# An encoder block on one core: four diagonals for the row of silu(c), h of a group made during the group ahead, modulation tiles spread one behind a weight tile, six half tiles in the ring

## The chip, the core and the metric

The kernel runs on one core of a Trainium2 chip. The metric is device time in microseconds (us) of one execution: 1720.41 us, the median of three runs (1719.41 to 1721.68). Five engines work side by side, each through its own queue in order: PE (matrix products; PEld is its weight load), DVE and ACT (elementwise), POOL (idle here) and SP, which here issues DMAs only.

## The reference, cut to what matters

```
mod = silu(c) @ W_ada + b_ada          # six rows of 2048: sh1, sc1, gt1, sh2, sc2, gt2
h   = rmsnorm(x, g_pre_mix) * (1 + sc1) + sh1          # x is 256 x 2048
proj = h @ w_in                        # 2048 x 10752: HGRN2 q, f, b, v, g; attention q, k, v; gates a, b
y = (sigmoid(gate_a) * (hgrn2(..) @ w_branch_a) + sigmoid(gate_b) * (attention(..) @ w_branch_b)) @ w_out
x = x + gt1 * rmsnorm(y, g_post_mix)
h = rmsnorm(x, g_pre_ffn) * (1 + sc2) + sh2
x = x + gt2 * rmsnorm(16 experts, each on the 32 tokens it picks, g_post_ffn)
```

All weights come from HBM once, in float32.

## The kernel before, in words

**Tiles.** Every weight is cut into tiles of 128 x 2048 float32 (1 MB). `stream` lists them in the order of `prog`, and `take` gives each a slot of `Mem` and issues its DMA on SP. `Mem` has 27 slots of 8 KB a partition, for tiles of weights and for everything else, handed out in the order in which they were freed in the program; a DMA waits until the slot's last user is through.

**Two sorts of tiles in the front part.** A modulation tile ("A" for sh1 and sc1, "B" for the other four rows) is used once on DVE: `ada` (L392) multiplies it by CR, the row of silu(c), and sums. A weight tile ("W" for w_in, "YA", "YB", "O" for the branch and output weights) is split by `split` into a high part (ACT, L426) and a rest (DVE, L427), in two halves. A half takes a slot of a ring (`NHL` of the 27 slots, 4 here). `finish` multiplies: 48 products 256 columns wide, or 24 of 512. It runs `LAH` weight tiles behind the split, 1 here.

**Order of the work.** CR is made first (`expand`: four times a diagonal on DVE L282, a product with ones on PE, a copy on ACT L293; one buffer for the diagonal), then x is normed and transposed into nT. h is made by `make_h` in four groups of four 128-row blocks, since the first ten chunks of w_in ("early": f0, b0, f1, b1, q0, q1, hg0, hg1, v0, v1) are gone through once for each group. Between groups the partial sums rest in SBUF: ACT copies them out of PSUM (L783) and in again (L780). h of a group needs its eight A tiles: `mod_gain` (L397, L399), then scale (ACT L409), high part (ACT L410) and rest (DVE L411). At a group's head the program finishes all products in flight before it makes h. After the groups come 44 "late" weight tiles, in whose time HGRN2 and then attention run as generators (`run_bg`, four steps after each weight tile), then 32 tiles of the branches and of the output (`dlist`). Before: in groups 0 to 2 eight A tiles among the first nine weight tiles, in group 3 eight B tiles; 38 B tiles among the late ones; the last 18 in the first 18 of `dlist`.

**Experts.** After a short stretch of norms and routing on small tiles, 16 experts of 24 tiles each are streamed through.

A scheduler puts the instructions into the engines' queues, so that their order differs a little from the program's.

Of the kernel before, what the change touches and what calls it, by code (L numbers as in the profile page):

```python
# [14 lines left out]
F32 = mybir.dt.float32  # L15
# [11 lines left out]
H = 8  # L27
# [3 lines left out]
EPS = 1e-6  # L31
ATT_SCALE = 128 ** -0.5
NEG = -3.0e38
BL = 0.87
BE = 8
BD = 18
NHL = 4
BG = 4
GRP = [4, 4, 4, 4]
NA0 = 1  # L40
HK = 1
LAH = 1


COLS = {}
# [80 lines left out]
def block_kernel(ctx: ExitStack, tc: tile.TileContext, x, cols, pos, ident_in, hmask, smask, w_ada, w_in, w_a, w_b, w_out, w_r, w_gu, w_dn, out):  # L126
    nc = tc.nc
    V, S, E = nc.vector, nc.scalar, nc.tensor
# [3 lines left out]
    mem = Mem(sp, 27)  # L132
    hring = Ring(mem, NHL)
    PS = pp.tile([128, 4096], F32, name="PS")
# [8 lines left out]
    def bank():  # L143
        ring["m"] = (ring["m"] + 1) % 3
        return PS[:, 2048 + 512 * ring["m"]:2560 + 512 * ring["m"]]
# [18 lines left out]
    pairs = []  # L164

    def latest(engine):
        for i in reversed(nc.cur_bb.bb.instructions):
            if i.engine == engine:
                return i
# [8 lines left out]
    def mm(o, l, r, start, stop, **kw):  # L178
        E.matmul(o, l, r, start=start, stop=stop, skip_group_check=True, **kw)  # L179
# [7 lines left out]
    def col(n, a=0, b=None):  # L187
        lo, hi = COLS[n]
        t, o = (ct0, 0) if lo < NCOL0 else (ct, NCOL0)
        return t[:, lo - o + a:(hi if b is None else lo + b) - o]  # L190
# [15 lines left out]
    def tiny(n):  # L206
        a = spos[0]
        spos[0] += n
        assert spos[0] <= SMW
        return small[:, a:a + n]  # L210

    def table(name="natural_log_exp_and_others"):

        S.preload_act_table_set(name)

    def rsqrt(ss, n):

        l, r, t, v = tiny(n), tiny(n), tiny(n), tiny(n)
        S.activation(l, ss, AF.Ln, scale=1.0 / D, bias=epsc)
        S.activation(r, l, AF.Exp, scale=-0.5)  # L220
        V.tensor_scalar(v, ss, 1.0 / D, EPS, ALU.mult, ALU.add)
        V.tensor_tensor(t, r, r, ALU.mult)
        V.scalar_tensor_tensor(t, t, -0.5, v, ALU.mult, ALU.mult)
        V.scalar_tensor_tensor(r, t, 1.5, r, ALU.add, ALU.mult)
        return r


    NG = len(GRP)
    G0 = [sum(GRP[:g]) for g in range(NG)]
    prog = [("X",)]  # L230
    a_tiles = [("A", p, k) for k in range(KT) for p in range(2)]
    b_tiles = [("B", p, k) for p in range(2, 6) for k in range(KT)]
    prog += a_tiles[:2 * GRP[0]]
    for g in range(NG):
        prog.append(("H", g))
        if g < NG - 1:
            todo = a_tiles[2 * G0[g + 1]:2 * G0[g + 1] + 2 * GRP[g + 1]]
        else:
            todo = b_tiles[:BE]
            b_tiles = b_tiles[BE:]  # L240
        nt, ne = len(todo), len(EARLY)
        for i, n in enumerate(EARLY):
            prog.append(("W", n, G0[g], GRP[g]))
            k = min(nt, (i + 1) * nt // (ne - NA0)) - min(nt, i * nt // (ne - NA0))
            prog += todo[:k]
            todo = todo[k:]
        prog += todo
    def mix(items, n, m):

        nonlocal prog, b_tiles  # L250
        n = min(n, len(b_tiles))
        for i, it in enumerate(items):
            prog.append(it)
            k = min(n, (i + 1) * n // m) - min(n, i * n // m)
            prog += b_tiles[:k]
            b_tiles = b_tiles[k:]

    late = [("W", n, 4 * q, 4) for n in LATE for q in range(4)]
    mix(late, int(BL * len(late) + 0.5), len(late))
    dlist = []  # L260
    for c in range(4):
        dlist += [("YA", c, q) for q in range(2)] + [("YB", c, q) for q in range(2)]
    dlist += [("O", c, q) for c in range(4) for q in range(4)]
    mix(dlist, len(b_tiles), BD)

    def src(it):
        k = it[0]
# [12 lines left out]
    def spread(c4, w, b=None):  # L280

        V.tensor_tensor(w, ident[:, None, :].to_broadcast([128, 4, 128]),  # L282
                        c4[:, :, None].to_broadcast([128, 4, 128]), ALU.mult)
        b = bank() if b is None else b
        mm(b, ones, w.rearrange("p a b -> p (a b)"), True, True)
        return b

    def expand(c16, name):

        r = mem.get([D], F32, name)  # L290
        w = mem.get([4, 128], F32, "diag")
        for c in range(4):
            S.copy(r[:, 512 * c:512 * c + 512], spread(c16[:, 4 * c:4 * c + 4], w))  # L293
        mem.put(w)
        return r

# [5 lines left out]
    def hk(tl, kt):  # L302
        return tl[kt // 8][:, kt % 8, :]
# [3 lines left out]
    S.activation(sig, col("c"), AF.Sigmoid)  # L307
    V.tensor_tensor(sig, sig, col("c"), ALU.mult)
    CR = expand(sig, "crow")
    X = [mem.get([D], F32, "x") for _ in range(NT)]  # L310
    ssq = tiny(NT)

    def norm_x():
        for tt in range(NT):
            nc.sync.dma_start(X[tt], x[tt])
        scr = mem.get([D], F32, "sq")
        for tt in range(NT):
            S.activation(scr, X[tt], AF.Square, accum_out=ssq[:, tt:tt + 1])
        mem.put(scr)
        rs = rsqrt(ssq, NT)  # L320
        for k2 in range(8):
            if k2 % 2 == 0:
                for tt in range(NT):
                    xp = X[tt][:, 256 * k2:256 * k2 + 512]
                    S.activation(xp, xp, AF.Copy, scale=rs[:, tt:tt + 1])
            b = bank()
            for j in range(2):
                for tt in range(NT):
                    E.transpose(b[:, 256 * j + 128 * tt:256 * j + 128 * tt + 128],
                                X[tt][:, 128 * (2 * k2 + j):128 * (2 * k2 + j) + 128], ident)  # L330
            S.copy(NTl[k2 // 4][:, 2 * (k2 % 4):2 * (k2 % 4) + 2, :].rearrange("p a b -> p (a b)"), b)
        mem.put(*X)

# [56 lines left out]
    def ada(p, k, t):  # L390

        V.scalar_tensor_tensor(t, t, 1.0, CR, ALU.mult, ALU.mult, accum_out=MOD[:, p, k:k + 1])  # L392
        mem.put(t)

    def mod_gain(p, ks):
        m = MOD[:, p, ks]
        V.tensor_tensor(m, m, bada[:, p, ks], ALU.add)  # L397
        if p in (1, 4):
            V.scalar_tensor_tensor(m, m, 1.0, col("gpm" if p == 1 else "gpf")[:, ks], ALU.add, ALU.mult)  # L399
        elif p in (2, 5):  # L400
            V.tensor_tensor(m, m, col("gqm" if p == 2 else "gqf")[:, ks], ALU.mult)

    def make_h(g):
        ks = slice(G0[g], G0[g] + GRP[g])
        mod_gain(0, ks)
        mod_gain(1, ks)
        for kt in range(ks.start, ks.stop):
            n = hk(NTl, kt)
            S.activation(n, n, AF.Identity, scale=MOD[:, 1, kt:kt + 1], bias=MOD[:, 0, kt:kt + 1])  # L409
            S.copy(hk(HH, kt), n)  # L410
            V.tensor_tensor(hk(HL, kt), n, hk(HH, kt).bitcast(F32), ALU.subtract)  # L411
            if kt % 2:
                yield
        if g == NG - 1:
            mem.put(*NTl)
# [57 lines left out]
    def late_tiles(names):  # L473
        for n in names:
            OT[n] = mem.get([8, 256], F32R, n)
# [149 lines left out]
    def attn_pre():  # L625
        AQ, AKV = SL["AQ"], SL["AKV"]
        late_tiles(("BH", "BL"))
        V.memset(SC, NEG)
# [15 lines left out]
    def attn(h):  # L644
# [40 lines left out]
        S.copy(OT["BH"][:, h, :], b[:, :256])  # L685
        V.tensor_tensor(OT["BL"][:, h, :], b[:, :256], OT["BH"][:, h, :].bitcast(F32), ALU.subtract)
        yield
# [6 lines left out]
        "YA": (lambda k: OT["OH"][:, k, :], lambda k: OT["OL"][:, k, :]),  # L694
        "YB": (lambda k: OT["BH"][:, k, :], lambda k: OT["BL"][:, k, :]),
        "O": (lambda k: hk(MH, k), lambda k: hk(ML, k)),
# [71 lines left out]
    def finish(it, parts):  # L768
# [29 lines left out]
        elif k in ("YA", "YB"):  # L798
# [11 lines left out]
            if q == 1:  # L810
# [6 lines left out]
                else:  # L817
# [3 lines left out]
                    if c == 3:  # L821
                        table()
                        mem.put(OT["OH"], OT["OL"], OT["BH"], OT["BL"])
        else:
# [23 lines left out]
    last_b = [it for it in prog if it[0] == "B"][-1]  # L848
    LA = LAH
    pend = []  # L850
    hs = iter(())
    for it in prog:
        if it[0] == "H":
            while pend:
                finish(*pend.pop(0))
            hs = make_h(it[1])
            for _ in range(HK):
                next(hs)
            continue
        if it[0] == "X":  # L860
            norm_x()
            rotary()
            continue
        t = take()
        if it[0] in "AB":
            ada(it[1], it[2], t)
            if it[0] == "B" and it[2] % 4 == 3:
                mod_gain(it[1], slice(it[2] - 3, it[2] + 1))
            if it == last_b:
                mem.put(CR)  # L870
            if it == ("B", 4, KT - 1):
                router_consts()
        else:
            pend.append((it, split(t)))
            for _ in hs:
                pass
            while len(pend) > LA:
                finish(*pend.pop(0))
            run_bg(BG)
# [117 lines left out]
    for e in range(NE):  # L997
# [9 lines left out]
        for k in range(KT):  # L1007
            w = take()
# [201 lines left out]
```

## Time and profile before

| | |
|---|---|
| median of 3 runs | 1720.41 us |
| the profiled execution | 1721.07 us, its span 1719.3 us |
| PE busy | 1437.4 us (84%) |
| DVE busy / ACT busy | 775.7 us (45%) / 555.7 us (32%) |
| moved by DMA | 633.57 MB, 369 GB/s over the span |
| chain that ended last | PE 47%, DMA 44%, DVE 5%, ACT 2% |

The span is the time from the first to the last instruction; times of the trace count from its start. A share over the whole span mixes stages: the front part (to 757 us), the routing (to 790 us) and the experts. PEclk is the granted TensorE clock as a share of full speed.

### The profile page before, as it was taken

What the parts mean: (1) busy time and instruction counts of PE and PEld (TensorE: products, weight loads), DVE (VectorE), ACT (ScalarE), POOL (GpSimd) and SP (SyncE); (2) the same over time, 40 slices, a digit from 0 to 9 for tenths busy, and PEclk for the clock granted to TensorE, in tenths of its full rate; (3) what the DMA queues carried; (4) which work ended last, traced back from release to release, by engine and by line L of the source; (5) the groups of instructions that cost most, each with busy time, mean ns of one, the idle gap of its engine ahead of it and who ended that gap; (6) DMA issues with size and microseconds to landing.
All of it is one profiled execution on the core that took longest, in us unless ns stands there. A gap on an engine that the chain in (4) does not pass through costs nothing.

```text
span 1719.3 us, 21982 instructions
## 1 busy us (share of the span) xinstructions
PE 1437.4 (84%) x9114; PEld 866.6 (50%) x9114; DVE 775.7 (45%) x1060; ACT 555.7 (32%) x858; POOL 0.2 (0%) x4
## 2 busy tenths in 40 slices
PE   4999999999999999997877777776777777687777
PEld 2989998778888888862322222221222222132123
DVE  6767787999997898442111101110110111011113
ACT  6467786665565444441200100100010011001003
POOL 0000000000000000000000000000000000000000
PEclk9999999999999999998988878878897989887888
DMA  9988955787979899767999999999999999999995
GB/s 384 418 338 326 361 218 202 271 312 269 363 296 365 331 420 399 276 266 306 418 419 420 420 420 419 420 420 419 418 419 419 420 420 420 419 420 419 418 419 233
DMA packets 88659, 633.57 MB, mean 369 GB/s; under 512 B 10096, under 2 KB 10480, under 8 KB 11760
## 3 DMA queue, kind: packets, MB, share of 16 engines
q1 hardware_dynamic: 88128, 631.39, 90.7%
q8 instruction: 71, 1.16, 0.3%
q10 hardware_dynamic: 432, 0.79, 0.1%
q14 instruction: 28, 0.23, 0.0%
HBM read 630.04 MB, written 2.10 MB: 368 GB/s over the span
## 4 chain that ended last, share of the span: by engine, by line
PE 47%; DMA 44%; DVE 5%; ACT 2%; issue 1%; SPq 0%; ACTq 0%; DVEq 0%
PE PS L179 45%; DMA w<-in_w_gu_dram 34%; DMA w<-in_w_dn_dram 9%; DVE w L392 2%; DVE hl L427 1%; ACT ew L1051 1%; DMA w<-in_w_in_dram 1%; PE PS L1024 0%; DMA w<-in_w_ada_dram 0%; ACT hl L426 0%; PE PS L903 0%; ACT ew L1021 0%; DVE F L500 0%; PE PS L678 0%; PE PS L760 0%
## 5 line engine op out<-in xcount | busy, mean ns | idle before, releaser
L179 PE MATMUL PS<-w,rt 128*32 128x512 f32 x2048 | 327.2, 717 | 141.2 <-DMA w<-in_w_gu_dram 139.5
L427 DVE TENSOR_TENSOR hl<-w,hl 128x1024 fp32r<-128x1024 f32 x232 | 280.8, 1222 | 107.7 <-ACT hl L426 107.3
L179 PE MATMUL PS<-hl,hl 128*128 128x256 f32 (+1 forms) x928 | 311.5, 336 | 0.0
L426 ACT CAST hl<-w 128x1024 fp32r<-128x1024 f32 x232 | 241.7, 1050 | 157.1 <-PE PS L179 146.8
L179 PE MATMUL PS<-hl,hh 128*128 128x512 f32 x832 | 267.9, 398 | 4.0 <-DVE hl L427 4.0
L179 PEld LDWEIGHTS PS<-w,rt 128*32 128x32 f32 x2048 | 54.7, 116 | 371.3 <-DMA w<-in_w_gu_dram 305.8
L392 DVE SCALAR_TENSOR_TENSOR w<-w,crow 128x2048 f32<-128x2048 f32 x96 | 218.8, 2284 | 4.6 <-ACT crow L293 2.8
L179 PE MATMUL PS<-ew,rt 128*128 128x256 f32 x512 | 155.8, 431 | 60.1 <-ACT ew L1051 60.1
L1062 DVE TENSOR_TENSOR acc<-acc,PS 128x512 f32<-128x512 f32 x120 | 82.5, 688 | 268.6 <-PE PS L179 268.6
L179 PE MATMUL PS<-hh,hl 128*128 128x256 f32 x1024 | 189.4, 287 | 12.5 <-ACT hl L426 8.3
L179 PEld LDWEIGHTS PS<-hl,hl 128*128 128x128 f32 x928 | 178.8, 193 | 16.5 <-issue 1.0
L179 PEld LDWEIGHTS PS<-hl,hh 128*128 128x128 f32 x832 | 154.8, 188 | 37.5 <-DVE hl L427 5.9
L179 PEld LDWEIGHTS PS<-hh,hl 128*128 128x128 f32 x1024 | 163.5, 196 | 13.7 <-ACT hl L426 8.7
L179 PE MATMUL PS<-w,ew 128*32 128x256 f32 x2048 | 152.0, 420 | 13.9 <-DVE ew L1030 13.9
L179 PEld LDWEIGHTS PS<-ew,rt 128*128 128x128 f32 x512 | 93.5, 202 | 134.0 <-ACT ew L1051 119.9
L1051 ACT COPY ew<-PS 128x256 f32<-128x256 f32 x128 | 47.6, 372 | 259.2 <-PE PS L179 259.2
L1030 DVE TENSOR_TENSOR ew<-ew,PS 128x256 f32<-128x256 f32 x16 | 6.7, 422 | 234.1 <-ACT ew L1029 234.1
L963 DVE TENSOR_SCALAR rt<-ct,rt,small 128x32 f32<-128x32 f32 x32 | 9.4, 300 | 214.8 <-PE PS L179 214.7
L179 PEld LDWEIGHTS PS<-w,ew 128*32 128x32 f32 x2048 | 57.4, 117 | 87.4 <-issue 49.0
L969 ACT COPY ew<-PS 128x512 f32<-128x512 f32 x15 | 8.8, 586 | 273.4 <-PE PS L179 273.4
L1021 ACT COPY ew<-PS 128x512 f32<-128x512 f32 x16 | 9.4, 586 | 234.1 <-PE PS L179 234.1
L179 PE MATMUL PS<-hl,mh 128*128 128x512 f32 x256 | 80.9, 396 | 0.0
(242 smaller groups left out, 1114.0 us busy)
## 6 DMA issues: line engine op xcount, KB each, us to landing
w<-in_w_gu_dram SPq DMA_DIRECT2D x256, 1024.0 KB, 19.9
w<-in_w_dn_dram SPq DMA_DIRECT2D x128, 1024.0 KB, 19.9
w<-in_w_ada_dram SPq DMA_DIRECT2D x96, 1024.0 KB, 8.1
w<-in_w_in_dram SPq DMA_DIRECT2D x84, 1024.0 KB, 7.4
w<-in_w_out_dram SPq DMA_DIRECT2D x16, 1024.0 KB, 11.1
w<-in_w_a_dram SPq DMA_DIRECT2D x8, 1024.0 KB, 10.0
w<-in_w_b_dram SPq DMA_DIRECT2D x8, 1024.0 KB, 11.8
x<-in_x_dram SPq DMA_DIRECT2D x4, 1024.0 KB, 9.4
```

The lines of the kernel that those rows point to most:

```text
L179: E.matmul(o, l, r, start=start, stop=stop, skip_group_check=True, **kw)
L392: V.scalar_tensor_tensor(t, t, 1.0, CR, ALU.mult, ALU.mult, accum_out=MOD[:, p, k:k + 1])
L426: S.copy(hl[:, 0, :], w)
L427: V.tensor_tensor(hl[:, 1, :], w, hl[:, 0, :].bitcast(F32), ALU.subtract)
L963: V.tensor_scalar(oh[:, tt, :], io, pm3[:, tt, e:e + 1], r2[:, tt:tt + 1], ALU.is_equal, ALU.mult)
L969: S.copy(g, b)
L1021: S.copy(gu, b)
L1030: V.tensor_tensor(he, sl_, b3[:, :, 64:128], ALU.mult)
L1051: S.copy(EW[:, 2, 256 * (cb % 2):256 * (cb % 2) + 256], b[:, :256])
L1062: V.tensor_tensor(acc(cb), acc(cb), p3, ALU.add)
```

## The change

Four things. `expand` has a buffer for each of its four diagonals. The ring has six half tiles and `finish` runs two weight tiles behind the split. h of group g+1 is begun after the eighth weight tile of group g and goes on by two blocks with each of its last two weight tiles (`next(hs)`), with nothing flushed ahead; h of group 0 is held behind the split of the first weight tile, and the second square of x behind the copies of CR. The modulation tiles follow at most one behind a weight tile: ten in each of the four groups (8 A and 2 B, in the last 10 B), 12 behind the first 30 late tiles, 14 behind the other 14, 8 behind the first 16 of `dlist`, 14 behind the next 14.

```diff
-BL = 0.87
-BE = 8
-BD = 18
-NHL = 4
+BE = [2, 2, 2, 10]
+BL = [(30, 12), (14, 14)]
+BD = [(16, 8), (14, 14)]
+NHL = 6
-NA0 = 1
-HK = 1
-LAH = 1
+NH0 = 3
+LAH = 2
@@ prog
-        prog.append(("H", g))
+        todo = b_tiles[:BE[g]]
+        b_tiles = b_tiles[BE[g]:]
         if g < NG - 1:
-            todo = a_tiles[2 * G0[g + 1]:2 * G0[g + 1] + 2 * GRP[g + 1]]
-        else:
-            todo = b_tiles[:BE]
-            b_tiles = b_tiles[BE:]
+            todo = a_tiles[2 * G0[g + 1]:2 * G0[g + 1] + 2 * GRP[g + 1]] + todo
         for i, n in enumerate(EARLY):
             prog.append(("W", n, G0[g], GRP[g]))
-            k = min(nt, (i + 1) * nt // (ne - NA0)) - min(nt, i * nt // (ne - NA0))
+            if g == 0 and i == 0:
+                prog.append(("H", 0))
+            k = min(nt, (i + 1) * nt // ne) - min(nt, i * nt // ne)
             prog += todo[:k]
             todo = todo[k:]
+            if g < NG - 1 and i == ne - NH0:
+                prog.append(("H", g + 1))
@@ expand
-        w = mem.get([4, 128], F32, "diag")
+        w = mem.get([4, 4, 128], F32, "diag")
         for c in range(4):
-            S.copy(r[:, 512 * c:512 * c + 512], spread(c16[:, 4 * c:4 * c + 4], w))
+            S.copy(r[:, 512 * c:512 * c + 512], spread(c16[:, 4 * c:4 * c + 4], w[:, c]))
@@ norm_x
+        pairs.append((latest(mybir.EngineType.Activation), crow_done))
@@ the loop over prog
         if it[0] == "H":
-            while pend:
-                finish(*pend.pop(0))
-            hs = make_h(it[1])
-            for _ in range(HK):
-                next(hs)
+            hs, hg_ = make_h(it[1]), it[1]
+            if it[1] == 0:
...
+                for _ in hs:
+                    pass
             continue
...
             pend.append((it, split(t)))
-            for _ in hs:
-                pass
+            if it[0] == "W" and it[2] < G0[hg_]:
+                next(hs, None)
+            else:
+                for _ in hs:
+                    pass
```

**Place 1: ACT at the start.** nT holds x normed and transposed; hh is the high part of h, hl the halves of a weight tile w. Before:

```order
L331 COPY nT_82<-PS 128x512 x2
L409 ACTIVATE nT_81<-nT_81,MOD 128x256 x2
L410 CAST hh_83<-nT_81 128x256 x2
L426 CAST hl_236<-w_234 128x1024
L426 CAST hl_239<-w_234 128x1024
```

Now:

```order
L337 COPY nT_82<-PS 128x512 x2
L432 CAST hl_227<-w_225 128x1024
L432 CAST hl_230<-w_225 128x1024
L415 ACTIVATE nT_81<-nT_81,MOD 128x256 x2
L416 CAST hh_83<-nT_81 128x256 x2
L415 ACTIVATE nT_81<-nT_81,MOD 128x256 x2
L416 CAST hh_83<-nT_81 128x256 x2
```

The first weight tile's two halves went ahead of h of group 0.

**Place 2: ACT from group 0 to group 1.** Q takes the sums of v0 and then of v1, the last two chunks of group 0; F is f0's, the first chunk of group 1; w_800, w_814 and w_762 are group 1's first tiles. Before:

```order
L426 CAST hl_802<-w_800 128x1024
L410 CAST hh_83<-nT_81 128x256
L426 CAST hl_805<-w_800 128x1024
L409 ACTIVATE nT_81<-nT_81,MOD 128x256 x2
L410 CAST hh_83<-nT_81 128x256
L783 COPY Q_77_559<-PS 128x1024
L410 CAST hh_83<-nT_81 128x256
L426 CAST hl_816<-w_814 128x1024
L426 CAST hl_819<-w_814 128x1024
L780 COPY PS<-F_44_256 128x1024 x2
```

Now:

```order
L415 ACTIVATE nT_81<-nT_81,MOD 128x256
L789 COPY HG_643<-PS 128x1024
L416 CAST hh_83<-nT_81 128x256
L432 CAST hl_698<-w_696 128x1024
L432 CAST hl_701<-w_696 128x1024
L789 COPY Q_78_512<-PS 128x1024
L786 COPY PS<-F_52_270 128x1024
L432 CAST hl_764<-w_762 128x1024
L432 CAST hl_767<-w_762 128x1024
L789 COPY Q_85_573<-PS 128x1024
```

All of h now stands ahead of the last tile's split (w_696), and the copy that brings f0's sums back into PSUM ahead of the copy that takes v1's sums out.

**Place 3: SP in the output products.** Before:

```order
L160 DMA w_5356<-in_w_out_dram 128x2048
L160 DMA w_5388<-in_w_out_dram 128x2048
L160 DMA w_5420<-in_w_out_dram 128x2048
L160 DMA w_5456<-in_w_out_dram 128x2048
L160 DMA w_5491<-in_w_out_dram 128x2048
```

Now:

```order
L159 DMA w_5506<-in_w_ada_dram 128x2048
L159 DMA w_5509<-in_w_out_dram 128x2048
L159 DMA w_5541<-in_w_ada_dram 128x2048
L159 DMA w_5544<-in_w_out_dram 128x2048
L159 DMA w_5580<-in_w_ada_dram 128x2048
L159 DMA w_5585<-in_w_out_dram 128x2048
```

Twelve modulation tiles that were loaded earlier now stand between the tiles of w_out, ahead of the first expert's.

## Rows read from the trace of the kernel before

**Rows 1.** Busy time by stage; columns of all such tables in the first line.

```profile
core 0: us, PE busy (x) PEld busy (x) DVE busy (x) ACT busy (x) POOL busy (x), PEclk, DMA share, GB/s
103.00:283.00 180.00, 180.00 (x1324) 172.94 (x1324) 135.26 (x135) 131.81 (x148) 0.00 (x0) 0.98 0.78 298
283.00:400.00 117.00, 111.59 (x576) 88.89 (x575) 114.33 (x152) 76.71 (x107) 0.00 (x0) 1.00 0.70 265
400.00:520.00 120.00, 119.98 (x578) 97.05 (x577) 116.93 (x188) 73.10 (x129) 0.00 (x0) 1.00 0.79 301
667.00:757.50 90.50, 90.50 (x395) 72.88 (x394) 45.23 (x44) 36.70 (x47) 0.00 (x0) 1.00 0.73 286
757.50:790.50 33.00, 18.51 (x98) 8.44 (x102) 21.48 (x62) 11.46 (x35) 0.00 (x0) 0.74 0.71 287
850.00:1700.00 850.00, 627.25 (x4474) 212.44 (x4476) 122.17 (x212) 77.37 (x196) 0.00 (x0) 0.84 1.01 417
```

**Rows 2.** Timeline of SP, 676 to 800 us: start, length, engine, line, DMAs.

```profile
757.91 16.23 SPq L160 DMA_DIRECT2D w<-in_w_dn_dram  x8
791.45 24.16 SPq L160 DMA_DIRECT2D w<-in_w_gu_dram  x16
```

**Rows 3.** Busy time just ahead of the first expert's products.

```profile
782.00:791.00 9.00, 5.85 (x32) 1.88 (x36) 5.28 (x17) 0.96 (x2) 0.00 (x0) 0.67 0.01 5
```

**Rows 4.** Timeline of the start; idle time before and what ended it in brackets.

```profile
5.03 2.08 PE L179 MATMUL PS<-diag,ones 128*128 128x512 f32 x2 [5.03 <-DVE diag L282]
7.73 1.91 ACT L318 ACTIVATE sq<-x 128x2048 f32<-128x2048 f32 x1 [4.88 <-DMA x<-in_x_dram]
16.69 0.59 ACT L293 COPY crow<-PS 128x512 f32<-128x512 f32 x1 [2.34 <-PE PS L179]
17.31 2.29 DVE L392 SCALAR_TENSOR_TENSOR w<-w,crow 128x2048 f32<-128x2048 f32 x1 [2.77 <-ACT crow L293]
36.64 1.09 ACT L409 ACTIVATE nT<-nT,MOD 128x256 f32<-128x256 f32 x2 [4.95 <-DVE MOD L399]
37.63 0.69 ACT L410 CAST hh<-nT 128x256 fp32r<-128x256 f32 x2
38.23 1.99 ACT L426 CAST hl<-w 128x1024 fp32r<-128x1024 f32 x2
39.33 0.58 PE L179 MATMUL PS<-hh,hl 128*128 128x256 f32 x1 [8.26 <-ACT hl L426]
```

**Rows 5.** SP's issues from 12.71 us; first weight tile's time to landing.

```profile
12.71 2.83 SPq L160 DMA_DIRECT2D w<-in_w_in_dram  x2
w<-in_w_in_dram SPq DMA_DIRECT2D x1, 1024.0 KB, 19.9
```

**Rows 6.** Timeline from group 0 to group 1, ACT and then PE.

```profile
98.82 1.01 ACT L783 COPY Q<-PS 128x1024 f32<-128x1024 f32 x1
100.03 1.99 ACT L426 CAST hl<-w 128x1024 fp32r<-128x1024 f32 x2
101.92 1.96 ACT L780 COPY PS<-F 128x1024 f32<-128x1024 f32 x2
102.99 0.58 PE L179 MATMUL PS<-hh,hl 128*128 128x256 f32 x1 [4.21 <-ACT PS L780]
```

**Rows 7.** Busy time across that wait, and in one microsecond after it.

```profile
98.80:108.50 9.70, 5.51 (x26) 5.51 (x27) 7.60 (x9) 5.07 (x6) 0.00 (x0) 0.66 0.97 389
105.00:106.00 1.00, 1.00 (x7) 1.00 (x6) 1.00 (x3) 0.00 (x0) 0.00 (x0) 0.50 0.82 328
```

**Rows 8.** The page's costliest groups: DVE's use of a modulation tile.

```profile
L392 DVE SCALAR_TENSOR_TENSOR w<-w,crow 128x2048 f32<-128x2048 f32 x96 | 218.8, 2284 | 4.6 <-ACT crow L293 2.8
```

**Rows 9.** Waits of PE from 283 to 400 us: total, times, longest.

```profile
PE PS L179 <- DVE hl L427: 4.0, 5, 1.4
PE PS L179 <- DVE F L523: 1.4, 2, 0.9
```

**Rows 10.** A weight tile loaded alone, issued at 276 us: time to landing.

```profile
w<-in_w_in_dram SPq DMA_DIRECT2D x1, 1024.0 KB, 4.8
```

More of the change, by code (lines that the diff above doesn't have):

```diff
@@ L243, in block_kernel, with mix @@
             prog.append(("W", n, G0[g], GRP[g]))
-            k = min(nt, (i + 1) * nt // (ne - NA0)) - min(nt, i * nt // (ne - NA0))
+            if g == 0 and i == 0:
+                prog.append(("H", 0))
+            k = min(nt, (i + 1) * nt // ne) - min(nt, i * nt // ne)
             prog += todo[:k]
             todo = todo[k:]
+            if g < NG - 1 and i == ne - NH0:
+                prog.append(("H", g + 1))
         prog += todo
-    def mix(items, n, m):
+    def mix(items, plan):
         nonlocal prog, b_tiles
[L251 to L256, printed above, removed]
+        for m, n in plan:
+            for i in range(m):
+                prog.append(items.pop(0))
+                k = (i + 1) * n // m - i * n // m
+                prog += b_tiles[:k]
+                b_tiles = b_tiles[k:]
+        prog += items
     late = [("W", n, 4 * q, 4) for n in LATE for q in range(4)]
-    mix(late, int(BL * len(late) + 0.5), len(late))
+    mix(late, BL)
     dlist = []
@@ L263, in block_kernel @@
     dlist += [("O", c, q) for c in range(4) for q in range(4)]
-    mix(dlist, len(b_tiles), BD)
+    mix(dlist, BD)
+    assert not b_tiles
     def src(it):
@@ L309, in block_kernel @@
     CR = expand(sig, "crow")
+    crow_done = latest(mybir.EngineType.Activation)
     X = [mem.get([D], F32, "x") for _ in range(NT)]
@@ L850, in block_kernel @@
     pend = []
-    hs = iter(())
+    hs, hg_ = iter(()), 0
     for it in prog:
         if it[0] == "H":
-            while pend:
-                finish(*pend.pop(0))
-            hs = make_h(it[1])
-            for _ in range(HK):
-                next(hs)
+            hs, hg_ = make_h(it[1]), it[1]
+            if it[1] == 0:
+                n, p = len(nc.cur_bb.bb.instructions), latest(mybir.EngineType.Activation)
+                for _ in hs:
+                    pass
+                pairs += [(i, p) for i in nc.cur_bb.bb.instructions[n:] if i.engine == mybir.EngineType.Activation]
             continue
```

## The prediction

> **What bounds the kernel now.** I read the busy time by stage first, then the timelines at the seams between the stages, then the waits of PE.
>
> By stage [rows 1] the kernel has two halves. Up to 757 us PE is the bound: from 667 to 757.5 us it is busy 90.50 of 90.50 us with DMA at 0.73; from 103 to 283 us it is busy 180.00 of 180.00. From 850 to 1700 us it is the other way round: DMA share 1.01 at 417 GB/s, PE 627 of 850. So a tile of 1.0486 MB takes 1.0486/417 = 2.51 us there, and the experts' end is set by when their stream can begin to run without a break.
>
> The seam between the halves says what a gain in the front part is worth. SP issues the first 24 tiles of the experts until 757.91 + 16.23 = 774.1 us, and the next only at 791.45 [rows 2]; from 782 to 791 us the DMA share is 0.01 [rows 3]. DMA there waits for slots, and slots come free only when PE has used the first expert tiles. The 33 us from the last output product at 757.5 us to the first expert product [rows 1] are small dependent steps which the change leaves alone. So each microsecond by which the front part ends earlier moves the experts, and with them the end, by one microsecond, as long as those 24 tiles are still there in time.
>
> What PE can win in the front part is its idle time. There are three such places. The start: its first group product begins at 39.33 us [rows 4]. The passage from group 0 to group 1: 4.21 us idle, and after it the granted clock is 0.50, the lower of its two levels (1.2 GHz), for the products up to about 108.5 us [rows 6, 7]. And the first part of the late weight tiles: 117.00 - 111.59 = 5.41 us from 283 to 400 us [rows 1], all of it behind DVE: 4.0 us on the second half of a split (hl) and 1.4 us on the HGRN step that makes F [rows 9]. DVE is busy 114.33 of these 117 us.
>
> **The change part by part, from the profiled execution's 1721.07 us** (0.66 above the median of the runs shown, a difference that I carry over).
>
> *Start.* PE makes one diagonal's two products in 2.08 us at 5.03 [rows 4]. With one buffer each diagonal waits for the products of the one before it, and CR's last copy ends at 16.69 + 0.59 = 17.28 us. With four buffers the products can follow one another: 5.03 + 4 x 2.08 = 13.35, and one copy, 0.59: 13.9 us, and I put the first modulation tile on DVE at 14.1 instead of 17.31, with ACT's other work between the copies. The second square of x (1.91 us) now stands behind the copies; behind it are the norm and transposing of x, which nobody needs before MOD is there. Before, MOD is ready at 36.64, when ACT begins to scale with it [rows 4], 19.3 us after 17.31, and eight tiles of 2.28 us [rows 8] are 18.3 of these: DVE has no gap to speak of. Shifted by 3.2 us MOD is ready at 33.4. The DMAs would allow it: the first weight tile, the ninth of these tiles, lands at 12.71 + 19.9 = 32.6 us [rows 5], so the eighth tile is there at about 30.1 and used by 32.4. Now the added wait decides: h of group 0 is held behind that tile's two high parts, 1.99 us [rows 4]: 32.6 + 1.99 = 34.6. Behind it on ACT stand scale and high part of two blocks, 1.09 + 0.69 = 1.8 us. The first products can begin when one of the two blocks is done, and run freely a little later: I take 36.5 instead of 39.33, a gain of 2.8. Bounds: nothing (if the weight tile lands 3 us later, since SP's queue is the same) and 4 (if h of one block is enough).
>
> *Passage between groups.* ACT takes v1's sums out at 98.82 (1.01 us), casts the next weight tile at 100.03 (1.99), and brings F in at 101.92 (two halves, 1.96); PE waits 4.21 us, to 102.99 [rows 6]. All products had been finished before h was begun. Now the order on ACT is h first (all four blocks ahead of the last tile's split), then F's sums in ahead of v1's sums out, and two weight tiles' products are in hand while this is done. The 4.21 us go. The 26 products that follow fill the 5.51 us of PE's work [rows 7]; at 2.4 GHz they would take half of it, 2.75, and by the mean product of the next stage, 180/1324 = 0.136 us [rows 1], 26 x 0.136 = 3.5. I take 3.1, so 2.4 less. Sum 6.6, bounds 0 and 7. What could be late next is MOD of group 1: its eight modulation tiles and two more stand among the first ten weight tiles of group 0 and h is begun after the eighth, so ACT's queue could stop at h for a tile of DVE's work, 2.28 us [rows 8].
>
> *Late tiles.* Behind the first 30 late weight tiles stood 26 modulation tiles; now 12. That takes 14 x 2.284 = 32.0 us [rows 8] off DVE where, from 283 to 520 us, it is 97 to 98% busy [rows 1]. The 5.41 us of PE's waiting have DVE as their only cause, and PE now also has two split tiles in hand instead of one. I take 4.0 back, since a wait on the HGRN step itself (1.4 us) need not go with it. Bounds: 5.4 above. Below, the ring's two further slots are taken from the loads: 27 - 6 = 21 slots instead of 23 for everything else. By the names in the code HGRN2's stretch keeps 17 of them in use (3 for h and CR, 8 and 3 and 1 for its halves' sums, temporaries and A/Q), so 4 are left for tiles on their way instead of 6. The nearest row is a tile loaded alone, 4.8 us from issue to landing [rows 10]; a tile's slot is freed by the split, two tiles ahead of the products. If one such refill lay bare in each of the four HGRN half passes, 4 x 4.8 = 19.2 us would be lost. I go by the idle time, since a late tile's products with its background work last some 7 us and with lookahead of two cover one refill of 4.8.
>
> *Other modulation tiles.* The groups take 8 more, 8 x 2.28 = 18 us of DVE, where PE is never idle between 103 and 283 us and DVE is busy 135 of 180 [rows 1]: hidden, since 45 us are free. The branch and output products take 22 instead of 18, and 14 instead of 2 stand behind the last 16, where DVE is 45 of 90.5 busy [rows 1]: 12 x 2.28 = 27 us, hidden. But they are also 12 x 2.51 = 30 us of DMA, ahead of the first expert's tiles in SP's queue. From 667 to 790.5 us DMA is busy 0.73 x 90.5 + 0.71 x 33 = 89.5 us of 123.5 [rows 1]; 30 more make 119.5. It fits by 4 us. I cost it at nothing; if that cover is gone, each missing tile costs 2.51 us.
>
> Sum: 2.8 + 6.6 + 4.0 = 13.4 us. 1721.07 - 13.4 = 1707.7 in the profiled execution, 1720.41 - 13.4 = 1707.0 as a median.
>
> **Rivals.** *A: the passage keeps its stall.* PE still stands when a group ends, since h of the next group waits for MOD, or F's copies for the buffer that v1's sums leave. For it: ACT works in order, and h, split and copies are all on it; against it: the new order has the copies of F ahead. Then 2.8 + 4.0 = 6.8 are left: 1713.6.
>
> *B: the DMAs are the bound already at the seam.* The 34 us that DMA idles around the routing are what the moved tiles use up, and slots may hold transfers back there. If five of the 24 expert tiles are not in by the first expert product, 5 x 2.51 = 12.5 us come back: 1720.41 - 13.4 + 12.5 = 1719.5, no change. For it: a margin of 4 us only; against it: share 0.01 at 782 to 791 us [rows 3], room that exists now. The Trainium skill ("Perfetto Trace Analysis", section "Identifying the Most-Contended Engine") would have one work on the most loaded engine first and judge DMA by bandwidth; 633.57 MB in 1719 us, 369 GB/s, against 417 at best here, makes that DMA, and by this rule an easier front part is worth little. The trace agrees for 850 to 1700 us and not for the front part, where DMA is at 0.70 to 0.79 [rows 1].
>
> *C: slower, HGRN2's stretch runs out of slots.* With 4 free slots instead of 6, a weight tile and the modulation tile behind it stand in SP's order, and a modulation tile that waits for DVE holds the weight tiles behind it. Four bare refills, 19.2 us, against 2.8 + 6.6 = 9.4: +9.8, or 1730.2. It decides from two refills on (9.6 us). For it: 2 of 6 slots gone, and background work that takes buffers in bursts; against it: DMA is at 0.70 there [rows 1], no wait of PE on a weight tile's DMA stands among its waits from 283 to 400 us [rows 9], and fewer modulation tiles need slots there. The Trainium skill ("Perfetto Trace Analysis", section "Optimization Strategy") says that the same gap repeating on the engine that should be saturated can mean too little SBUF for the next tile; the rows show gaps with DVE as their end, so this is not yet so before the change, but it speaks against giving two more slots to the ring.
>
> **How the numbers follow.** The forecast, 1707, has a chance of 0.63 (its own range 1702 to 1712: the terms' upper bounds give 4 + 7 + 5.4 = 16.4, so 1704, and 2 more for what rows do not show; on the other side half of the passage and 2 of the late tiles may stay). A has 0.11, B 0.11, C 0.15. Range 1702 to 1721: it takes in A and B and leaves out C and little below. About 0.2%, 3.4 us, is what a measurement of this kernel can tell from no change; so faster is forecast and A, 0.74, same is B, 0.11, slower is C, 0.15.
>
> **What would show it.** Right: the first group product at 36 to 37 us; where group 1 begins, near 96 us, no idle time of PE over 1 us and no granted clock of 0.50; DVE clearly less busy and PE nearly gapless in the late tiles; the last output product near 744 and the first expert product near 777 us; 417 GB/s from there to the end. Wrong: DMA share near 1.0 right up to the first expert product with expert products waiting for w (B); waits of PE or ACT on a weight tile's DMA in the HGRN stretch (C); a PE wait on ACT's copies at a group's head (A).

## The result, and the profile after

The changed kernel takes 1704.67 us (median of 4 runs, 1704.39 to 1705.82) against 1719.91 us for the kernel before in the runs at its side: 15.2 us less, ratio 0.9911 (95% interval 0.99 to 0.9923). The prediction was 1707.0 us. The profiled execution took 1704.93 us, its span 1703.1; before, 1721.07 and 1719.3.

The stages after, columns as in [rows 1]:

```profile
core 0: us, PE busy (x) PEld busy (x) DVE busy (x) ACT busy (x) POOL busy (x), PEclk, DMA share, GB/s
35.80:37.80 2.00, 1.99 (x9) 1.99 (x10) 2.00 (x4) 2.00 (x6) 0.00 (x0) 0.50 1.03 418
39.80:41.80 2.00, 2.00 (x17) 2.00 (x16) 2.00 (x3) 0.00 (x0) 0.00 (x0) 0.90 1.02 422
98.00:108.00 10.00, 10.00 (x86) 10.00 (x85) 8.69 (x7) 6.41 (x8) 0.00 (x0) 1.00 1.01 419
283.00:400.00 117.00, 115.78 (x617) 93.43 (x616) 108.55 (x160) 75.74 (x108) 0.00 (x0) 1.00 0.56 205
742.50:775.00 32.50, 18.00 (x95) 7.93 (x94) 21.22 (x62) 11.65 (x36) 0.00 (x0) 0.74 0.87 356
```

From 98 to 108 us, where PE had waited 4.21 us and then worked at 0.50 [rows 6, 7], it is now busy without a gap at 1.00. From 283 to 400 us it idles 1.22 us instead of 5.41. Around the routing DMA idles 0.13 of 32.5 us, 4.2 us.

The timeline of the start after, to set beside [rows 4]:

```profile
5.06 6.00 PE L178 MATMUL PS<-diag,ones 128*128 128x512 f32 x8 [5.06 <-DVE diag L286]
13.84 2.28 DVE L398 SCALAR_TENSOR_TENSOR w<-w,crow 128x2048 f32<-128x2048 f32 x1
32.48 1.99 ACT L432 CAST hl<-w 128x1024 fp32r<-128x1024 f32 x2 [4.36 <-DMA w<-in_w_in_dram]
34.38 1.09 ACT L415 ACTIVATE nT<-nT,MOD 128x256 f32<-128x256 f32 x2
35.81 0.80 PE L178 MATMUL PS<-hh,hl 128*128 128x256 f32 x2 [8.31 <-ACT hh L416]
```

The four diagonals' products follow one another, the first modulation tile is used at 13.84 instead of 17.31 us, and ACT begins with the weight tile, which lands at 32.5 us. Group products begin at 35.81.

ACT at the passage from group 0 to group 1, to set beside [rows 6]:

```profile
95.05 1.01 ACT L789 COPY Q<-PS 128x1024 f32<-128x1024 f32 x1 [1.44 <-PE PS L178]
96.10 1.02 ACT L786 COPY PS<-F 128x1024 f32<-128x1024 f32 x1
97.05 1.99 ACT L432 CAST hl<-w 128x1024 fp32r<-128x1024 f32 x2
100.80 1.02 ACT L789 COPY F<-PS 128x1024 f32<-128x1024 f32 x1 [1.76 <-PE PS L178]
```

The sums of group 0's last chunk go out at 95.05, those of group 1's first at 100.80: 5.75 us, as between most chunks. Before it was 98.82 to 111.61, 12.79.

PE's waits from 283 to 400 us, against [rows 9]:

```profile
PE PS L178 <- DVE F L529: 0.9, 1, 0.9
PE PS L178 <- DVE T L520: 0.3, 1, 0.3
```

And SP at the seam, against [rows 2]:

```profile
689.85 54.15 SPq L159 DMA_DIRECT2D w<-in_w_gu_dram  x16
744.04 14.23 SPq L159 DMA_DIRECT2D w<-in_w_dn_dram  x8
776.22 23.90 SPq L159 DMA_DIRECT2D w<-in_w_gu_dram  x16
```

All 24 tiles are issued by 758.3 us, and SP goes on at 776.22 instead of 791.45: the experts begin 15.2 us earlier.

Four landmarks of each trace cut the span into stages that add up: when ACT first takes f0's sums out of PSUM (*start*), from there to v0's of group 3 (*groups*), from there to the end of the last output product (*late tiles and output*), and what is left (*rest*: routing, experts, tail). PSUM is where PE leaves its products. In us, one trace of every kernel of this study, beside the median of its runs (the traced run can be some 3 us off its median: old plan took 1717.1, 25 slots 1715.1):

| kernel | median | start | groups | late, output | rest |
|---|---|---|---|---|---|
| before | 1719.9 to 1720.8 | 47.59 | 223.71 | 486.20 | 961.8 |
| after | 1704.67 | 43.82 | 216.73 | 482.14 | 960.4 |
| one diagonal | 1709.15 | 47.23 | 216.73 | 482.42 | 961.9 |
| h at the head | 1707.91 | 44.41 | 219.98 | 482.28 | 958.7 |
| old plan | 1713.91 | 43.68 | 226.27 | 482.56 | 962.8 |
| ring of four | 1708.16 | 43.61 | 216.92 | 485.42 | 960.3 |
| no hold | 1706.89 | 47.02 | 216.73 | 482.32 | 958.9 |
| more at the end | 1705.13 | 43.66 | 216.73 | 484.40 | 958.7 |
| 25 slots | 1712.68 | 44.42 | 216.73 | 484.91 | 967.2 |
| warm PE | 1705.68 | 43.04 | 216.73 | 482.33 | 959.7 |
| before + diagonals | 1717.01 | 44.91 | 222.69 | 487.77 | 960.1 |
| before + ring | 1724.84 | 47.12 | 223.41 | 491.22 | 959.4 |
| before + h ahead | 1721.98 | 50.79 | 223.87 | 484.52 | 961.5 |
| before + plan | 1717.56 | 47.86 | 219.98 | 488.16 | 959.0 |

So of 16.2 us of span the start gave 3.8, the groups 7.0, the late tiles 4.1, the rest 1.4. The rest varies by some 4 us between kernels whose routing and experts are the same instructions (958.7 to 962.8, without the one with 25 slots), so its 1.4 us is not put down to anything. The other three columns are sharper: between kernels that have the same instructions there, the groups differ by 0.01 us (216.73 in six), the late tiles by some 0.3 (482.14 to 482.42), the start by 0.8 (43.61 to 44.42). The experiments are read by them, with these limits.

### The profile page after: what moved, and what is told of

It reads as the page before. It is cut to its first block, busy times and chain, and to the rows that moved or that the text cites. A ratio compares the mean times of both kernels' runs of the same rounds, so it can differ in the third digit from the quotient of the medians.

```text
span 1703.1 us, 21981 instructions
## 1 busy us (share of the span) xinstructions
PE 1421.2 (83%) x9114; PEld 857.5 (50%) x9114; DVE 775.7 (46%) x1060; ACT 555.6 (33%) x858; POOL 0.2 (0%) x4
## 4 chain that ended last, share of the span: by engine, by line
PE 50%; DMA 41%; DVE 4%; ACT 3%; issue 1%; SPq 0%; ACTq 0%; DVEq 0%
PE PS L178 49%; DMA w<-in_w_gu_dram 35%; DMA w<-in_w_dn_dram 5%; ACT ew L1061 1%; DMA w<-in_w_in_dram 1%; DVE hl L433 1%; DMA w<-in_w_ada_dram 1%; PE PS L1034 1%; DVE w L398 0%; ACT ew L1031 0%; DVE ew L1040 0%; PE PS L684 0%; ACT ew L1039 0%; PE PS L913 0%; DVE F L506 0%
## 5 line engine op out<-in xcount | busy, mean ns | idle before, releaser
L178 PE MATMUL PS<-w,rt 128*32 128x512 f32 x2048 | 333.7, 729 | 149.6 <-DMA w<-in_w_gu_dram 148.3
L432 ACT CAST hl<-w 128x1024 fp32r<-128x1024 f32 x232 | 238.0, 1049 | 148.1 <-PE PS L178 143.3
L178 PE MATMUL PS<-ew,rt 128*128 128x256 f32 x512 | 151.1, 420 | 60.1 <-ACT ew L1061 60.1
L178 PE MATMUL PS<-w,ew 128*32 128x256 f32 x2048 | 146.0, 406 | 15.4 <-DVE ew L1040 15.4
```

What stands on the lines that cost most here:

```text
L432: S.copy(hl[:, 0, :], w)
```

## Experiments

The first four undo one part each in the changed kernel, with everything else as changed.

**One diagonal.** In `expand`, `w = mem.get([4, 128], ...)` for all four.

> The changed kernel with one buffer for the four diagonals again; all else as changed. Theory (the diagonals' waits set the start): the row of silu(c) is ready at 17.3 instead of 11.7 us, the modulation row near 36.6 instead of 32.9, and since the first weight tile's high parts are then already made, scale and high part of two blocks follow at once: first group product near 38.4 instead of 35.8, so 2.6 us later, 1707.3. Rival (the order of the queues, h behind the first weight tile, made the gain): first product still at 35.8, 1704.7.

Measured 1709.15 us, the first group product at 38.98:

```profile
38.98 0.80 PE L178 MATMUL PS<-hh,hl 128*128 128x256 f32 x2 [5.04 <-ACT hh L416]
40.11 0.58 PE L178 MATMUL PS<-hl,hl 128*128 128x256 f32 x1 [0.33 <-DVE hl L417]
```

The start loses 3.4 us; groups and late tiles stay. The theory holds, a little larger than expected.

**h at the group's head.**

```diff
-            if g < NG - 1 and i == ne - NH0:
-                prog.append(("H", g + 1))
         prog += todo
+        if g < NG - 1:
+            prog.append(("H", g + 1))
@@ the loop over prog
+            if it[1] > 0:
+                while pend:
+                    finish(*pend.pop(0))
             hs, hg_ = make_h(it[1]), it[1]
+            if it[1] > 0:
+                next(hs)
```

> The changed kernel with h of groups 1 to 3 made at the group's head again, all products in hand finished ahead of it; ring, lookahead and plan as changed. Theory (making h during the group ahead takes the passage away): PE waits some 4 us at 95 to 100 us and works at half clock after it, 7 us are lost there, 1711.7. Rival (the passage went because the modulation tiles of the next group come one place earlier, or because of the lookahead): no wait there, 1704.7.

Measured 1707.91 us. The stall does not come back: in the waits of PE no wait for the sums' copies stands, and the groups lose 3.25 us in all, near one microsecond at each of the three passages. The theory for the passage is refuted by this run: something else had taken the stall away.

**Old plan.**

```diff
-BE = [2, 2, 2, 10]
-BL = [(30, 12), (14, 14)]
-BD = [(16, 8), (14, 14)]
+BE = [0, 0, 0, 8]
+BL = [(44, 38)]
+BD = [(18, 18)]
-            k = min(nt, (i + 1) * nt // ne) - min(nt, i * nt // ne)
+            k = min(nt, i + 1) - min(nt, i)
```

The second edit keeps the eight A tiles of a group behind its first eight weight tiles, which h, begun after the eighth, needs.

> The changed kernel with the old places of the 64 tiles of the other four rows: none in groups 0 to 2 and eight in group 3, 38 evenly behind the 44 late weight tiles, 18 behind the first 18 of the branch and output tiles. Theory (DVE's load in the late tiles was what PE waited for): the 4 us of the late stretch are lost again, with PE waits on the second half of a split, 1708.7. Rival (the deeper ring alone hides that): 1704.7.

Measured 1713.91 us, 9.2 us lost, but not where the theory put them: 9.5 are lost in the groups, and the late tiles only 0.4. PE waits at the end of groups 1 and 2 now. The first of these:

```profile
149.30 0.80 PE L178 MATMUL PS<-hl,hh 128*128 128x512 f32 x1 [2.89 <-ACT PS L786]
```

and ACT ahead of it:

```profile
145.44 1.99 ACT L432 CAST hl<-w 128x1024 fp32r<-128x1024 f32 x2
147.33 1.00 ACT L789 COPY Q<-PS 128x1024 f32<-128x1024 f32 x1
148.23 1.01 ACT L786 COPY PS<-Q 128x1024 f32<-128x1024 f32 x1
```

The copy that brings v1's sums in stands behind the high parts of a further weight tile; in the changed kernel it goes ahead of them, at 143.69. So DVE's load in the late tiles was not what PE paid for, once the ring is deep.

**Ring of four, lookahead of one.** `NHL = 4`, `LAH = 1`.

> The changed kernel with four half tiles in the ring and products one weight tile behind the split; plan and h as changed. Theory (the late stretch is won by DVE's smaller load): late stretch as in the changed kernel to within 1 us, and 1 or 2 us lost at the passage, since only one tile is in hand there: 1705 to 1707. Rival (the ring's depth wins the late stretch): the 4 us are lost there, 1708.7 or more.

Measured 1708.16 us: the groups keep all but 0.2 of their gain, the late tiles lose 3.3 of theirs. Here the rival was right in place and nearly in size. PE waits longest at the head of HGRN2, near 268 us: 2.0 us for a split that stands behind HGRN2's first instructions on ACT, and the granted clock falls:

```profile
PE PS L178 <- ACT hl L432: 2.0, 1, 2.0
PE PS L178 <- DVE hl L433: 0.4, 1, 0.4
262.00:283.00 21.00, 18.54 (x84) 14.25 (x83) 18.68 (x27) 17.45 (x23) 0.00 (x0) 0.92 0.32 119
```

In the changed kernel that wait is 0.6 us and the clock of the stretch 1.00. Two tiles are in hand there, and the split also stands a little earlier on ACT (265.49 instead of 266.88 us). Ring and lookahead were changed together in every run, so which of the two is needed is not shown.

The next four each put one part into the kernel before. Three of them change nothing else; + h ahead also needs other places for the modulation tiles.

**Before + diagonals.** The first edit of the diff above alone.

> The kernel before with four diagonal buffers and nothing else. Theory (the chain of the diagonals alone sets the start): modulation row near 33.4 instead of 36.6, scale and high part of two blocks ahead of the weight tile's first high part as before, so first group product near 36.1 instead of 39.3, 3.2 us: 1717.5. Rival (the gain at the start needs the weight tile's split ahead of h): under 1 us, 1720.

Measured 1717.01 us; the first group product at 35.78, as in the changed kernel:

```profile
35.78 0.58 PE L179 MATMUL PS<-hh,hl 128*128 128x256 f32 x1 [8.78 <-ACT hl L426]
43.00:45.00 2.00, 2.00 (x19) 2.00 (x18) 1.96 (x3) 0.10 (x1) 0.00 (x0) 1.00 1.02 422
41.00:43.00 2.00, 2.00 (x14) 2.00 (x13) 2.00 (x2) 1.05 (x1) 0.00 (x0) 0.68 0.98 406
```

The start gains 2.7 of 3.8 us. The other 1.1 are lost after the first product: the granted clock is at 1.00 only after some 42 us, against 40 in the changed kernel. That need not be a lack of the other edits. In h at the group's head, whose start is the changed kernel's, it is at 1.00 hardly sooner, near 41.7 us:

```profile
39.80:41.80 2.00, 2.00 (x12) 2.00 (x11) 2.00 (x3) 0.00 (x0) 0.00 (x0) 0.54 1.05 434
```

**Before + ring.** `NHL = 6`, `LAH = 2`.

> The kernel before with six half tiles in the ring and products two weight tiles behind the split, nothing else. Theory (from the run with h at the group's head and the run with the old plan: lookahead wins the late stretch, and goes far to take the first passage away): 3 to 4 us in the late tiles, and 6 us at the passage from group 0 to group 1: 1711. Rival (the passage needs the modulation tiles one place earlier or h ahead): its stall stays, 1717.

Measured 1724.84 us, 4 us slower than before, which neither expectation had. The passage keeps its stall (4.2 us for the sums' copies), and in the late tiles, where 2 to 6 us had been won at different points up to 528 us, one wait near 530 us takes back more:

```profile
SPq L160 <- PE PS L179: 5.0, 1, 5.0
523.25 0.91 SPq L160 DMA_DIRECT2D w<-in_w_in_dram  x2
530.64 1.06 ACT L814 ACTIVATE GB<-GB 128x1024 f32<-128x1024 f32 x1
531.60 1.05 ACT L814 ACTIVATE GA<-GA 128x1024 f32<-128x1024 f32 x1
533.62 0.79 PE L179 MATMUL PS<-hl,hh 128*128 128x512 f32 x1 [4.88 <-ACT hl L426]
531.00:535.50 4.50, 1.84 (x4) 1.02 (x5) 3.13 (x5) 4.50 (x6) 0.00 (x0) 0.50 0.85 319
```

SP stood 5.0 us, to 522.8, on the DMA of a modulation tile, a wait that ended with PE's products (the first line). Two weight tiles stood behind it in SP's order, went out from 523.25 on and took 6.9 and 8.9 us to land, the first near 530.2. ACT then had two activations of the gates ahead of the split, to 532.65. PE idled 4.88 us and then worked at 0.50: from one copy of GB to the next it took 29.05 us instead of 21.76, so 7.3 were lost. That is the mechanism of rival C once, a modulation tile that holds up the weight tiles behind it, with some 2 us of ACT's order on top.

**Before + h ahead.** The changed kernel with one diagonal, the old plan as in its own run, ring of four, lookahead of one, and h of group 0 ahead of the first weight tile without holds.

> The kernel before with h of groups 1 to 3 begun during the group ahead and nothing flushed, each group's eight modulation tiles one behind each of its first eight weight tiles (h needs them there); one diagonal, ring of four, lookahead one, the other rows' tiles in the old places. Theory (h ahead takes the first passage away by itself, and the later ones stay without loss): 7 us, 1713.4. Rival (as in the run with the old plan and the deep ring, the high parts of the next weight tiles stand on ACT ahead of the sums' copies, and some 4.6 us are lost at each of the two later passages): 7 - 9.2, so 1722.6.

Measured 1721.98 us. Its start is 3.2 us later, which the expectation had overlooked: all of h of group 0 stands ahead of the first split here, so the first group product comes at 41.02 us instead of 39.33, and PE waits once more, 1.67 us at 43.9. The first passage is free (102.01 to 107.77, 5.76 us), but PE waits 3.9 us for the sums' copies at the second:

```profile
PE PS L178 <- ACT PS L784: 3.9, 1, 3.9
```

The groups gain nothing in sum.

**Before + plan.** The three tables, `mix` and the spacing of the changed kernel, nothing else.

> The kernel before with the new places of the modulation tiles and nothing else. Theory (each part needs the others: undoing the plan cost 9 us, but much of that by the order in which ACT's work falls): the late tiles win 1 us (of the 4, ring and lookahead hold 3), the passage from group 0 to group 1 keeps its stall or hands it to a later group: 1717 to 1722. Rival (the plan is the main part of the gain): 1711 or less.

Measured 1717.56 us. ACT at the first passage:

```profile
99.14 1.01 ACT L783 COPY Q<-PS 128x1024 f32<-128x1024 f32 x1 [2.27 <-PE PS L179]
100.05 1.05 ACT L426 CAST hl<-w 128x1024 fp32r<-128x1024 f32 x1
101.00 1.02 ACT L780 COPY PS<-F 128x1024 f32<-128x1024 f32 x1
101.95 2.00 ACT L426 CAST hl<-w 128x1024 fp32r<-128x1024 f32 x2
105.36 1.02 ACT L783 COPY F<-PS 128x1024 f32<-128x1024 f32 x1 [1.41 <-PE PS L179]
```

No stall: 6.22 us from v1 to f0, though h is made at the head and everything is flushed. F's copy now comes behind one high part instead of two [rows 6]. The groups win 3.7 us, over half of the change's gain there. The late tiles lose 2.0 us with the ring of four, against a theory that had them win 1.

The last four test terms and rivals in the changed kernel.

**Warm PE.**

```diff
             norm_x()
+            for _ in range(7):
+                mm(obank[:, :256], ones, NTl[1][:, 7, :], True, True)
```

> The changed kernel with seven more products 256 columns wide on PE between the last transposing of x and the first group product, into a bank that nobody reads; nothing that is computed changes. In the changed kernel PE is idle from 27.5 to 35.8 us, and the first 4.2 us of group products run at a granted clock of 0.50. Theory (PE's idle time ahead lowers the clock): the group products start at the full clock, first chunk out at about 41.7 instead of 43.8 us, 2 us earlier, 1702.6. Rival (the low clock there does not depend on what PE did just before, or the first products wait for something else, the weight tile's parts): nothing gained, 1704.7; if the added products overrun, up to 1 us lost.

Measured 1705.68 us (1703.58 to 1706.23), no difference that these runs can tell from the changed kernel.

```profile
29.16 6.04 PE L178 MATMUL PS<-nT,ones 128*128 128x256 f32 x14 [0.68 <-ACT nT L337]
33.28 1.99 ACT L432 CAST hl<-w 128x1024 fp32r<-128x1024 f32 x2 [4.17 <-DMA w<-in_w_in_dram]
36.62 0.50 PE L178 MATMUL PS<-hh,hl 128*128 128x256 f32 x2 [1.42 <-ACT hh L416]
36.00:38.00 2.00, 1.38 (x9) 1.19 (x10) 2.00 (x4) 2.00 (x6) 0.00 (x0) 1.00 0.99 410
```

The clock is at 1.00 when the group products begin, as the theory said. But h is ready 0.8 us later in this run (the products wait 1.42 us for it), so 0.8 of the 2 us is left at the first chunk. The added products are not the reason: the first weight tile, which h is held behind, lands at 33.28 instead of 32.48 us, and it was issued 0.8 us later, at 13.39, long before them. Counted from its landing the first chunk is out 1.6 us sooner, near the theory's 2.

**More at the end.** `BL = [(30, 8), (14, 14)]`, `BD = [(16, 8), (14, 18)]`.

> The changed kernel with four modulation tiles moved from behind the first 30 late tiles to behind the last 14 output tiles (8 there instead of 12 behind late ones, 18 instead of 14 at the end). Theory (the DMAs fit the stretch from the last output products to the first expert product by some 4 us; in the changed kernel DMA idles 0.13 of 742.5 to 775 us, 4.2 us): 4 x 2.51 = 10 us more are asked of them, so the stream is late by 2 to 6 us: 1706.7 to 1710.7. Rival (the idle 14 us of DMA between 667 and 757 us take it): 1704.7.

Measured 1705.13 us (1704.44 to 1707.32): 10 us more of DMA at the end, and no loss that the medians can tell. DMA's share from 742.5 to 775 us is now full:

```profile
742.50:775.00 32.50, 18.82 (x103) 8.51 (x102) 20.00 (x58) 11.56 (x35) 0.00 (x0) 0.79 1.01 420
```

The 4 us of margin around the routing are used, and the rest is not longer (958.7), so at the seam the rival stands. The idle 14 us that it named are not in the changed kernel's trace, though: from 667 to 757 us its DMA share is 0.95, 4.5 us idle. And the late column is 2.3 us longer (484.40), more than it varies by: from 283 to 520 us PE idles 2.8 us instead of 1.2, in waits on HGRN2's and attention's steps and not on a tile's DMA. So in this trace the tiles that were moved cost something where they were taken away.

**25 slots.** `mem = Mem(sp, 25)`.

> The changed kernel with 25 slots of 8 KB instead of 27. Theory (HGRN2's stretch keeps some slack in slots, and lookahead covers one lone refill): under 1.5 us lost in the front part, 1706 at most. Rival (two slots fewer leave refills bare, as in the run with the ring alone, each some 5 us of waiting and 2 us of half clock): one to four of them, 1711 to 1732.

Measured 1712.68 us, 8 us slower, and both expectations missed the place. The late tiles lose 2.8 us, in which no wait for a tile's DMA shows; the rest loses 6.8 in the traced run:

```profile
748.59 33.65 SPq L159 DMA_DIRECT2D w<-in_w_dn_dram  x8
```

The 24th tile of the experts is issued at 782.2 us, 3.7 us after the first expert product (778.59), instead of 16.8 us ahead of it (758.3 and 775.09).

**No hold.** The line that adds the pairs for h of group 0 is left out.

> The changed kernel without the hold that keeps h of group 0 behind the first weight tile's high parts; the scale of two blocks now stands ahead of them on ACT and the high parts of h behind. Theory (ACT's order decides: 32.9 us for the modulation row, 1.1 of scale, 2.0 of casts, 0.7 of high parts): first group product near 36.5 instead of 35.8, 0.7 us later. Rival (the hold costs the time until the weight tile lands): first product earlier, near 35.0.

Measured 1706.89 us. The first group product comes at 37.07, near what was expected: 0.6 of the 1.3 us were lost before the edit could act (the first weight tile is issued at 13.21 instead of 12.59), the other 0.7 are the theory's. But the start loses 3.2 us:

```profile
37.07 0.80 PE L178 MATMUL PS<-hh,hl 128*128 128x256 f32 x2 [8.82 <-ACT hh L416]
38.55 0.58 PE L178 MATMUL PS<-hl,hl 128*128 128x256 f32 x1 [0.68 <-DVE hl L417]
41.00:43.00 2.00, 2.00 (x12) 2.00 (x11) 2.00 (x4) 0.00 (x0) 0.00 (x0) 0.50 1.01 418
```

PE waits 0.68 us just after the beginning, and the granted clock is still 0.50 at 43 us; it is back at 1.00 near 44.6.

## Why the prediction was right, and where its reasons were not

The sum was near because its sizes were read from idle time of PE that stood in the trace and that the change removed. For two of the three terms it was removed by something other than the sum said, and that the total still came out is luck to this extent.

**What a gain in the front part is worth: right.** The last output product ends 14.8 us earlier and the experts begin 15.2 us earlier, at the same seam of 32.4 us (before 32.8). The condition, that the 24 tiles are there in time, was tested from its other side by 25 slots.

**The start: right in mechanism, 1.0 us too small.** 3.8 us instead of 2.8. The weight tile landed as worked out (32.5 us). The first product came at 35.8 and not at 36.5, since h of one block was enough, which the sum had only as its upper bound. The diagonals are the main part: alone they bring 2.7 us, and without them the changed kernel loses 3.4. The step "Now the added wait decides" saw only a price in the hold. Without the hold the median is 2.2 us higher and the start 3.2 us longer: 0.6 was lost before the edit could act, 0.7 is ACT's order, the rest a gap of 0.68 us and a longer time at the lower clock, which varies between traces (last section). So the hold does not cost anything on balance; how much it gives is not shown. With one diagonal, where the hold stands too, the start is 0.4 us shorter than before, less than traces of the same start differ by.

**The passage: right in size, wrong in its cause.** 7.0 us in the groups against 6.6, all of it at this one passage (12.79 to 5.75 us). The sum put it down to h made ahead and to nothing being flushed. But h at the head with a flush costs 3.25 us, not 7, and the plan alone removes the stall and wins 3.7 us. With the new plan the two add up to the 7.0; with the old places of the B tiles h ahead wins nothing (before + h ahead), since the stall moves to a later passage.

What the kernels without a stall at the first passage share is that the eight modulation tiles of a group stand behind its first eight weight tiles; the three that keep it (before, + diagonals, + ring) have them one place later, behind the second to the ninth. This spacing alone was not run, and it is not enough by itself: in groups 1 and 2 of the kernel before it is the same, and their passages are free. DVE finishes MOD, then ACT takes v1's sums and f0's out, at the first passage ([rows 6] has the copy of v1's) and at the second:

```profile
88.94 0.17 DVE L399 SCALAR_TENSOR_TENSOR MOD<-MOD,ct 128x4 f32<-128x4 f32 x1
149.44 0.16 DVE L399 SCALAR_TENSOR_TENSOR MOD<-MOD,ct 128x4 f32<-128x4 f32 x1
162.78 1.02 ACT L783 COPY Q<-PS 128x1024 f32<-128x1024 f32 x1 [0.97 <-PE PS L179]
168.54 1.02 ACT L783 COPY F<-PS 128x1024 f32<-128x1024 f32 x1 [1.83 <-PE PS L179]
```

In the three traces with the stall MOD is finished 9.7 us ahead of the copy of v1's sums, and at every such passage without it, in all traces, 13.2 us or more ahead. So the likeliest cause is that MOD came too late, which put h's steps on ACT among the copies. No run moves MOD alone, so this is argued and not shown. What the rows show is that ACT's order goes with the wait: where the copy of sums stands behind one more tile's high parts, PE waits for it, and the passage costs 5 us (old plan, each of two) to 7 us (before, and before + h ahead). Rival A thus occurred, in kernels other than the changed one.

**The late tiles: right in size, wrong in its cause.** 4.1 us against 4.0. The step "have DVE as their only cause" read the name of the waiting's end as its cause. With 38 modulation tiles there as before, the deep ring and the lookahead keep 3.6 of the 4.1 us; with 12 behind the first 30 and the shallow ring 3.3 are lost, and the new plan alone, with the shallow ring, loses 2.0 against the kernel before. So ring and lookahead together bridged the waits, and DVE's load hardly mattered. That load was also a little overstated: by the table of the kernel before 25 tiles stood behind the first 30 late ones, not 26, so 13 were taken away, and DVE is busy 108.55 of 117 us there instead of 114.33.

**The other tiles at nothing: right.** Twelve more of them at the end cost nothing at the seam, and neither did four more, which used up the margin of 4 us that rival B went by. That the margin would have been the limit is thus not shown.

**Rival C was nearer than its chance of 0.15 says, but as an interaction.** The ring of six alone is slower than before by one wait of 4.88 us and the clock behind it. The refill took 6.9 us, against the 4.8 of a tile alone [rows 10], and ACT's order added to the wait. With the changed plan, or the old plan with h ahead, it does not occur. Whether fewer tiles waiting in SP's order or only another order of slots removes it is open.

## What to carry to other kernels

The gains of a change's parts need not add. Alone, + ring was 4 us slower and + h ahead 1 us slower, + diagonals 3.7 us faster and + plan 3.3; that makes 1.7 us in sum, and together the parts won 15.2. The changed kernel loses 3 to 9 us when any one of the four is undone. A wait's end tells which engine came last, not what would cure it. Runs that leave out one part, read by landmarks that cut the span into stages, come nearer to that. In a queue that works in order, look first at what stands one or two places ahead of the copy that another engine waits for.

## What was not expected of the hardware

How long the group products stay at a granted clock of 0.50 after they begin differed between traces by more than the edits explain. Where PE had no gap of over 0.1 us in that time, it was 3.4 us in before + ring, 4.4 in the changed kernel (35.8 to 40.2), 4.5 in the kernel before, 5.9 with h at the group's head and 6.5 in before + diagonals. With a gap it was 4.1 us (one diagonal, 0.33 us), 5.9 (before + h ahead, 1.67 us) and 7.6 (no hold, 0.68 us). So the longest of these times came with a gap, but that the gap made it is not shown. Products put ahead of the group products brought the clock to 1.00 in time (warm PE). And the routing, experts and tail took between 958.7 and 962.8 us in kernels where these are the same instructions.
